# A hybrid attention and RWKV-7 step on one core: three engines in a fixed order through the recurrence, the group norm in four stages, the triangular solve in four pieces

## The chip, the cores and the metric

The kernel runs on one NeuronCore of a Trainium2 chip, on its five engines: TensorE (PE, with its weight loads shown as PEld), VectorE (DVE), ScalarE (ACT), GpSimd (POOL) and SyncE (SP), which here issues nearly all transfers between HBM and the core's memory. The metric is the device time of one execution in microseconds (us), lower is better.

## The reference

One inference step of a two-layer trunk over a prompt of 2048 tokens, with 16 meta tokens in front, and over 8 decode sequences of 4 new tokens. Layer 0 is sliding-window attention, layer 1 is RWKV-7 time mixing. The change touches the last stage of layer 1: the recurrence, the group norm, the gate, the output projection and the last RMS norm.

```python
def wkv_scan(S0, r, w, k, v, a, b):
    # S_t = S_{t-1} diag(w_t) + (S_{t-1} a_t) b_t^T + v_t k_t^T ;  y_t = S_t r_t   (16 heads, S 64 x 64)
...
    S, y = wkv_scan(wkv0, r_h, w_h, k_h, v_h, -kk, kk * a_h)
    mean = jnp.mean(y, axis=-1, keepdims=True)
    var = jnp.mean(jnp.square(y - mean), axis=-1, keepdims=True)
    y = ((y - mean) * lax.rsqrt(var + GN_EPS)).reshape(B, T, R_WIDTH)
    y = y * ln_g + ln_b
    bonus = jnp.sum(r_h * k_h * r_k, axis=-1, keepdims=True) * v_h
    y = (y + bonus.reshape(B, T, R_WIDTH)) * jax.nn.silu(g)
    out = jnp.einsum('btw,wd->btd', y, w_out)
...
    h = h + y                      # residual, then the final rmsnorm(h) * final_gain
```

## The kernel before

The recurrence is done by chunks of 32 tokens. A token tile (`Unit` in the code) is 128 tokens, so four chunks; tile 0 holds the meta tokens in one chunk, tiles 1 to 16 hold the prompt, and the sample tokens run at the end. The attention layer, the projections of layer 1 and the decay factors lie ahead of this stage and leave their results in DRAM.

Inside a chunk, the token-by-token dependence is a triangular system per head. Its inverse is computed ahead, for a whole tile, and does not depend on the state:

- `scores(u, c2)` multiplies keys and queries for two chunks into PSUM (`pz`). ACT copies one part to `LAs` (four copies), DVE multiplies the rest by the masks `smk` back into the tile `L` (four instructions).
- `inverse(u)` writes `LAs` to DRAM (`la_d`), reads it back with the heads on partitions (`LA`), multiplies it by the norms `ln`, and runs 31 steps of two POOL instructions each: `XT` is an outer product, `X` takes it in by a sum. Step j works on (j//2 + 1) x (31 - j) columns. The result goes to DRAM (`tt_d`) and comes back as `TT`.
- `keys(u, c2)` transposes the decayed keys `BK` on PE into `kt`; ACT copies them to `LS` (eight copies).

`chain(u, ch)` is the recurrence proper, in three steps: PE multiplies `L` with `Z` (state and values) into `C`, and ACT copies it to `R0s`; PE multiplies `R0s` with `TT` (the solve) and ACT copies the result into `Z` (four copies); PE multiplies `LS` with `Z`, and DVE scales this into the next chunk's `Z` (four instructions `Z<-C,pe`). The next chunk's first product needs that `Z`. So from chunk to chunk there is one chain through PE, ACT, PE, ACT, PE and DVE.

Between these steps the loop over tiles and chunks gives out other work in small portions, by a budget of estimated microseconds: `project_out` of the tile two back (chunks 0 and 1, dense products `po`), `gate` of the tile one back (chunks 2 and 3, products `pd`, transposes `yps`, the halves `yp`), `group_norm` of the tile one back (chunks 0 and 1), `outputs` (the products `Y`), and `elementwise`, which loads, scores and starts the inverse of the tile two ahead.

`group_norm` sums `Y` on DVE, subtracts the mean, has ACT square (`ysq`), sums the squares, has POOL take the power -1/2 (`var`), and then runs on DVE the product with `var`, `lng`, `lnb`, and for each half a load `vt` of the values, its product with `bont`, and the sum. `project_out` ends with squares on ACT (`sq`), a power on POOL (`ms`) and the final product of `h` on DVE.

Who runs when: the program text gives an order ("traced" below), but a scheduler in the compiler lays out each engine's queue by its own timeline and the text's priorities. Some places bind it: `tc.issue_after(x)` queues what is traced inside it behind instruction x on x's engine, and `released()` does so for the latest chain instruction of each engine. Each engine, and SP's queue of transfers, then works through its queue in order and waits where an operand is not there.

Of the kernel before, what the change touches and what calls it, by code (L numbers as in the profile page):

```python
# [19 lines left out]
P = 128  # L20
D = 1024
KC = 8
# [8 lines left out]
def tile_hybrid_step(ctx: ExitStack, tc: tile.TileContext, a, o, c):  # L31
# [847 lines left out]
    def begin(idx, t, off, n, kind):  # L879
# [6 lines left out]
        u.blk, u.c0 = place[t][0], (place[t][1] + off) // 32  # L886
        return u

    def load_vectors(u):
# [65 lines left out]
    def inverse(u, room=None, ln=None):  # L955
# [62 lines left out]
    with ExitStack() as ph:  # L1018
# [144 lines left out]
        for x, b in enumerate(order):  # L1163
# [39 lines left out]
            if follow is None:  # L1203
# [11 lines left out]
                if nblk > 2:  # L1215
# [3 lines left out]
                    for i, x0, room in ((1, 0, room1), (0, 1024, None)):  # L1219
                        u = us[i]  # L1220
                        u.LAs = las[:64, x0:x0 + 256 * u.nch].rearrange("p (h c g i) -> p h c g i", h=2, g=4, i=32)
                        for c2 in range(u.np):
                            scores(u, c2)
                        inverse(u, room, las[:, x0 + 1024 - 32:x0 + 1024] if i == 0 else las[:, 1536:1568])
# [19 lines left out]
    with ExitStack() as ph:  # L1244
# [7 lines left out]
        SQ = 2  # L1252
        early = [0]

        def banks(u):
# [37 lines left out]

            return 32 * (1 - e + 2 * gh)

        def elementwise(u):
            load = idle() if u.L else load_vectors(u)
            next(load, None)
# [7 lines left out]
            if u.kind != "m":  # L1306
                u.bont = wk.tile([P, 16], F32, name="bont", tag="bont", bufs=4)
                dma(u.bont[:u.n], bo_d[u.idx])
            if u.tt_d is None:
                u.LAs = wk.tile([64, 2, u.nch, 4, 32], F32, name="LAs", tag="LAs", bufs=1)  # L1310
# [4 lines left out]
                inverse(u)  # L1315
            if u.kind != "s":
                u.TT = wp.tile([P, u.nch, 4, 32], F32, name="TT", tag=("sels", "l2t")[u.idx % 2])
            for gh in range(2):
                dma(u.TT[64 * gh:64 * gh + 64].rearrange("p c g i -> p (c g i)"), u.tt_d[:, gh:4:2].rearrange("k q x -> q k x"))
            yield 0.8  # L1320

        Zcount = [0]
# [224 lines left out]

        def group_norm(u):
            n = u.n
            if u.kind == "s":  # L1550
                u.ytm = u.Ys
            else:
                u.ytm = lt.tile([P, 2, 8, 64], F32, name="ytm", tag="ytm", bufs=1)
            y = u.ytm[:n].rearrange("p e g d -> p (e g) d")
# [3 lines left out]
            for e in range(2):  # L1558
                v_.tensor_reduce(out=mean[:n, e * 8:e * 8 + 8], in_=u.Y[e][:n], axis=AX.X, op=ALU.add)
                yield 0.6  # L1560
            v_.tensor_scalar(out=mean[:n], in0=mean[:n], scalar1=1.0 / 64, scalar2=None, op0=ALU.mult)
            if u.kind == "s":
                for e in range(2):
                    tt(v_, u.ytm[:n, e], u.Y[e][:n], mean[:n, e * 8:e * 8 + 8].unsqueeze(2).broadcast_to([n, 8, 64]), ALU.subtract)
            else:
                for x in range(2):
                    for e, ps_ in HS:
                        tt(v_, u.ytm[64 * x:64 * x + 64, e], u.Y[x][ps_],
                           mean[ps_, x * 8:x * 8 + 8].unsqueeze(2).broadcast_to([64, 8, 64]), ALU.subtract)
                    yield 0.9  # L1570
            for e in range(2):
                ysq = wk.tile([P, 8, 64], F32, name="ysq", tag="ysq", bufs=SQ)
                act(ysq[:n], u.ytm[:n, e], AF.Square)
                v_.tensor_reduce(out=var[:n, e * 8:e * 8 + 8], in_=ysq[:n], axis=AX.X, op=ALU.add)
                yield 0.6
            with tc.high_priority(offset=5000):
                g_.tensor_scalar(out=var[:n], in0=var[:n], scalar1=1.0 / 64, scalar2=64e-5, op0=ALU.mult, op1=ALU.add)
                tt(g_, var[:n], var[:n], mhalf[:n], ALU.pow)
            tt(v_, y, y, bc(var), ALU.mult)
            yield 1.1  # L1580
            yf = u.ytm[:n]
            tt(v_, yf, yf, lng[:n], ALU.mult)
            yield 1.1
            tt(v_, yf, yf, lnb[:n], ALU.add)
            yield 1.1
            for e in range(2):
                vt = wk.tile([P, 8, 64], F32, name="vt", tag="ysq", bufs=SQ)
                dma(vt[:n].rearrange("p g d -> p (g d)"), v_d[u.t][u.cols, e, :])
                tt(v_, vt[:n], vt[:n], u.bont[:n, 8 - e * 8:16 - e * 8].unsqueeze(2).broadcast_to([n, 8, 64]), ALU.mult)
                tt(v_, u.ytm[:n, e], u.ytm[:n, e], vt[:n], ALU.add)  # L1590
                yield 1.2

# [5 lines left out]
        def gate_dense(u, ch, room=None):  # L1598

            n = u.n  # L1600
            if ch == 0:
# [8 lines left out]
            u.gt = gt = wk.tile([P, 512], F32, name="gt", tag="ysq", bufs=SQ) if room is None else room[:, ch]  # L1610
# [24 lines left out]
        def project_out(u, ch):  # L1635
# [10 lines left out]
                                   lambda kc, part: u.yp[kc // 4][:, part, kc % 4, :])  # L1646
            stt(h1[:n, sl], ps[:n], 0.5 / WSC, h1[:n, sl], ALU.mult, ALU.add)
            yield MARK
            sq = wk.tile([P, 512], F32, name="sq", tag="ysq", bufs=SQ)
            act(sq[:n], h1[:n, sl], AF.Square, accum_out=u.ssq[:n, ch:ch + 1])  # L1650
            if ch == 1:
                ms = wk.tile([P, 2], F32, name="ms2", bufs=2)
                with tc.high_priority(offset=5000):
                    g_.tensor_scalar(out=ms[:n], in0=u.ssq[:n], scalar1=1.0 / D, scalar2=0.5e-6, op0=ALU.mult, op1=ALU.add)
                    tt(g_, ms[:n, 0:1], ms[:n, 0:1], ms[:n, 1:2], ALU.add)
                    tt(g_, ms[:n, 0:1], ms[:n, 0:1], mhalf[:n, 0:1], ALU.pow)
                stt(h1[:n], h1[:n], ms[:n, 0:1], fg[:n], ALU.mult, ALU.mult)
                if t == 0:
                    dma(o["y_sample"].rearrange("b t d -> (b t) d"), h1[:32])
# [36 lines left out]

        room_v[0] = pf
        PLAN = {(1, 2): [2], (1, 3): [3], (2, 0): [4], (2, 1): [5], (2, 2): [6], (2, 3): [7]}
        side, rests = [], []

        def after_rhs():

            for gen in rests:
                run(gen)
            with released():
                for fn in side:
                    fn()
            del side[:], rests[:]

        def side_work(u, ch, ahead, last):  # L1710
            if u.kind == "p":
# [10 lines left out]
        for i, u in enumerate(us):  # L1722
# [2 lines left out]
            if i > 2:  # L1725
                pe[0], pe[1] = project_out(us[i - 2], 0), project_out(us[i - 2], 1)
            if i > 1:
                norm = group_norm(us[i - 1])
                ew[0] = ew[1] = norm
                pe[2], pe[3] = gate(us[i - 1], 0), gate(us[i - 1], 1)  # L1730
            if i < 2:
                pe = [rest_v] * 4
            soon = i + 3 if i < 1 else i + 2
            ahead = elementwise(us[soon]) if soon < len(us) and i != 1 else idle()
            for ch in range(u.nch):
# [3 lines left out]
                with released() if i == 0 else ExitStack():  # L1739
                    next(rec)  # L1740
                after_rhs()
                run(ew[ch], 1.2)
                run(pe[ch], VB.get((i, ch), (1.2, 1.9))[0])
                next(rec)
# [151 lines left out]
```

## Time and profile before

| | |
|---|---|
| median of 3 runs | 2650.34 us (2645.37 to 2650.36) |
| the profiled execution | 2649.89 us, its span 2648.1 us |
| PE busy | 2243.8 us, 85% of the span |
| DVE busy | 1677.2 us, 63% |
| ACT busy | 1171.9 us, 44% |
| POOL busy | 1042.4 us, 39% |
| first and last copy of a chunk's R0s | at 1609.9 and 2544.0 us |

In rows of a timeline the columns are: start in us, duration in us, engine, line, operation, output and inputs by name, shape, count, and in brackets the idle time before it with what ended it. In rows of waits: engine, line and output, "<-" what it waited for, total us, times, longest. In rows of groups: the busy total and the mean of one in ns, then the idle time before. In rows of windows: the stretch, its length, then busy us and count of PE, PEld, DVE, ACT and POOL, the granted TensorE clock, the DMA share and GB/s. "issue" means that the profile shows nothing that was waited for.

### The profile page before, as it was taken

The page shows a single profiled execution, that of the slowest core. Times are in us where ns is not written, and L with a number is a line of the kernel's source. Part 1 is how long each engine was busy: PE and PEld are TensorE (multiplying, and loading weights), DVE is VectorE, ACT ScalarE, POOL GpSimd, SP SyncE. Part 2 cuts the span into 40 slices and gives each one's busy share as a digit, 9 for nine tenths or more (in the row PEclk, how much of TensorE's full clock was granted, in tenths as well). Part 3 has the DMA queues.
Part 4 walks back from the last instruction along what each step waited for, and adds up shares of the span by engine and source line. Part 5 has one row for each costly group of instructions (what it writes and reads, how often), then busy time and mean ns, then how long its engine had stood idle before and what let it go on. Part 6 is the DMA issues. An engine that isn't in the chain of part 4 may idle for free.

```text
span 2648.1 us, 60911 instructions
## 1 busy us (share of the span) xinstructions
PE 2243.8 (85%) x24932; PEld 1549.0 (58%) x24932; DVE 1677.2 (63%) x3164; ACT 1171.9 (44%) x2799; POOL 1042.4 (39%) x1572
## 2 busy tenths in 40 slices
PE   7999899989999878999999995666777766777797
PEld 5877777768744446777666673444444444444453
DVE  6597666566839877665566665546556556556675
ACT  6676546555514335543434352333334433344332
POOL 4242113331204235433333342345555666556603
PEclk9999999999999989999999997788888988888898
DMA  8433212331466654322222244753444533445323
GB/s 201 126 105 106 81 53 88 120 116 43 156 165 224 208 186 140 98 92 96 85 97 88 77 130 122 203 152 98 112 115 115 143 99 98 117 122 123 85 62 82
DMA packets 346235, 312.99 MB, mean 118 GB/s; under 512 B 205546, under 2 KB 282218, under 8 KB 344131
## 3 DMA queue, kind: packets, MB, share of 16 engines
q1 hardware_dynamic: 344339, 305.30, 39.8%
q0 software_dynamic: 1616, 3.79, 0.6%
q8 instruction: 196, 3.21, 0.5%
q14 instruction: 84, 0.69, 0.1%
HBM read 191.15 MB, written 119.84 MB: 117 GB/s over the span
## 4 chain that ended last, share of the span: by engine, by line
PE 44%; DVE 17%; issue 12%; DMA 9%; ACT 9%; POOL 7%; SPq 3%; POOLq 0%; ACTq 0%; DVEq 0%
PE pd L38 25%; PE po L38 5%; PE C L38 4%; DVE xm L47 3%; DMA L<-ar 3%; SPq L50 3%; PE pz L38 2%; DVE xpr L44 2%; ACT ssb L41 2%; DMA wst<-in_rwkv_w_in 1%; PE sc L38 1%; POOL X L44 1%; PE Y L38 1%; PE oT L38 1%; PE kt L1353 1%
## 5 line engine op out<-in xcount | busy, mean ns | idle before, releaser
L38 PEld LDWEIGHTS <-yp 128*128 128x128 f16 x1488 | 138.5, 98 | 164.1 <-issue 7.5
L47 DVE SCALAR_TENSOR_TENSOR xm<-dx,mu,xn 128x256 f32<-128x256 f32 (+2 forms) x432 | 199.8, 522 | 54.1 <-POOL dx L44 52.9
L38 PE MATMUL C<-Z,L 128*32 128x64 f32 x2048 | 50.1, 249 | 215.5 <-issue 209.2
L44 POOL TENSOR_TENSOR XT<-LA,X 128x126 f32<-128x126 f32 (+24 forms) x458 | 192.7, 421 | 37.9 <-PE C L38 2.5
L44 POOL TENSOR_TENSOR X<-X,XT 128x126 f32<-128x126 f32 (+24 forms) x458 | 186.9, 408 | 34.9
L38 PE MATMUL pd<-wg,xg 128*128 128x512 f16 (+1 forms) x816 | 192.8, 384 | 1.0 <-DMA xg<-xg 1.0
L38 PE MATMUL pd<-xp,wq 128*128 128x256 f16 (+2 forms) x1728 | 184.1, 265 | 9.8 <-DVE qp L47 7.7
L38 PE MATMUL pd<-xp,wg 128*128 128x256 f16 (+2 forms) x1728 | 186.3, 269 | 0.5 <-DVE qp L47 0.4
L38 PE MATMUL pd<-wvv,xpr 128*128 128x512 f16 (+1 forms) x816 | 185.9, 385 | 0.0
L38 PE MATMUL pd<-xpr,w 128*128 128x256 f16 (+2 forms) x1728 | 185.5, 267 | 0.0
L38 PE MATMUL po<-wo,yp 128*128 128x512 f16 x768 | 184.4, 382 | 1.1 <-DVE yp L47 1.0
L38 PEld LDWEIGHTS C<-Z,L 128*32 128x32 f32 x2048 | 39.1, 127 | 240.7 <-issue 239.2
L38 PE MATMUL pd<-xpr,wkk 128*128 128x256 f16 (+2 forms) x1728 | 179.5, 264 | 0.0
L38 PEld LDWEIGHTS <-wq 128*128 128x128 f16 x1728 | 158.4, 98 | 30.4 <-DVE qp L47 8.9
L38 PEld LDWEIGHTS <-wg 128*128 128x128 f16 x1728 | 161.3, 100 | 23.1 <-issue 3.6
L44 POOL TENSOR_TENSOR ssb<-ssb,bias 128x512 f32<-128x512 f32 x64 | 86.3, 1355 | 224.5 <-DVE ssb L462 181.3
L41 ACT ACTIVATE R0s<-C 128x256 f32<-128x256 f32 x65 | 24.9, 383 | 335.0 <-PE C L38 334.3
L38 PEld LDWEIGHTS <-w 128*128 128x128 f16 x1728 | 157.3, 99 | 26.7 <-issue 9.7
L38 PEld LDWEIGHTS <-wkk 128*128 128x128 f16 x1728 | 158.3, 98 | 15.6 <-issue 0.4
L38 PE MATMUL pd<-w,yp 128*128 128x512 f16 x720 | 162.3, 383 | 3.2 <-DMA yp<-y 3.2
L44 POOL TENSOR_TENSOR ps<-wst,ps 128x1024 f16<-128x1024 f32 x32 | 69.4, 2168 | 221.7 <-ACT wst L41 198.3
L44 POOL TENSOR_TENSOR LA<-LA,ln 128x1024 f32<-128x1024 f32 x16 | 31.1, 1947 | 287.1 <-DMA LA<-la_d 240.7
(356 smaller groups left out, 4958.8 us busy)
## 6 DMA issues: line engine op xcount, KB each, us to landing
wst<-in_rwkv_w_in SPq DMA_DIRECT2D x32, 512.0 KB
wsp<-ps SPq DMA_DIRECT2D x32, 512.0 KB
BK<-bk SPq DMA_DIRECT2D x32, 512.0 KB
L<-ar SPq DMA_DIRECT2D x64, 256.0 KB
x<-in_x_prompt SPq DMA_DIRECT2D x29, 512.0 KB
xn<-xn SPq DMA_DIRECT2D x14, 1028.0 KB
ar<-aro SPq DMA_DIRECT2D x28, 512.0 KB
bk<-bko SPq DMA_DIRECT2D x28, 512.0 KB
```

Of the source, the lines that this page charges most:

```text
L38: return t_.matmul(out=out, lhsT=lhsT, rhs=rhs, start=start, stop=stop, **kw).ins
L41: return s_.activation(out=out, in_=in_, func=func, **kw).ins
L44: return e.tensor_tensor(out=out, in0=in0, in1=in1, op=op).ins
L47: v_.scalar_tensor_tensor(out=out, in0=in0, scalar=scalar, in1=in1, op0=op0, op1=op1)
L50: return nc.sync.dma_start(out=out, in_=in_).ins
L1353: t_.transpose(out=ps[:w * 64, j].rearrange("p e d -> p (e d)"), in_=u.BK[half][:, j, 2 * c2:2 * c2 + w, :].rearrange("p c x -> p (c x)"), ...
```

## The change

It rewrites the loop for tiles 2 to 14 (`steady`); tiles 0, 1, 15 and 16 keep the old loop, with small joints.

- `in_order()` is called at the end of every chunk. It ties each traced instruction of DVE, ACT and POOL to the one traced before it on the same engine, so these three run in the order of the text. PE and SP stay with the scheduler.
- `inverse` becomes a generator that stops before steps 8, 16 and 23. For the tile two ahead its first piece is traced in chunk 3, the other three in chunks 0, 1 and 2 of the next tile. The load of `TT` follows the last piece.
- The loads of the tile two ahead are traced in chunk 0 (`BK`, `pe`, `bont`, and the first `L`, unless it was loaded in chunk 3 before) and chunk 1 (the second `L`), its scores in chunks 1 and 2.
- `group_norm` runs in stages. In chunk 3 of the tile itself: the loads of `vt`, the mean of the first half, and the products of `vt` with `bont`. In chunk 0 of the next tile: the second mean, the subtractions, the squares and `var`. In chunk 1: the products with `var` and `lng`. In chunk 2: `lnb` and the sums with `vt`.
- `keys(u, 1)` is traced after the solve of chunk 0, `keys(u.next, 0)` after that of chunk 3.
- The last step of `project_out` is cut: squares and `ms` in chunk 2, the final product of `h` in chunk 3.
- `ysq` and `sq` are written to PSUM instead of SBUF, `vt` and `gt` have buffers of their own, and the scratch for POOL's own transfers shrinks from 4096 to 2048.

```diff
@@ inverse
         for j in range(low, 31):
+            if j in (8, 16, 23):
+                yield
...
@@ group_norm
+            if u.kind != "s":
                 for e in range(2):
+                    vt = wk.tile([P, 8, 64], F32, name="vt", tag="vt", bufs=2)
+                    dma(vt.rearrange("p g d -> p (g d)"), v_d[u.t][u.cols, e, :])
+                    vts.append(vt)
+                yield MARK
...
+                if vts and x == 0:
+                    for e in range(2):
+                        tt(v_, vts[e], vts[e], u.bont[...].broadcast_to([n, 8, 64]), ALU.mult)
+                    yield MARK
...
-                ysq = wk.tile([P, 8, 64], F32, name="ysq", tag="ysq", bufs=SQ)
+                ysq = u.Y[e] if u.kind != "s" else wk.tile([P, 8, 64], F32, name="ysq", tag="vt", bufs=2)
...
+            yield MARK
             tt(v_, y, y, bc(var), ALU.mult)
             yield 1.1
             tt(v_, yf, yf, lng[:n], ALU.mult)
-            yield 1.1
+            yield MARK
             tt(v_, yf, yf, lnb[:n], ALU.add)
...
@@ project_out
-            sq = wk.tile([P, 512], F32, name="sq", tag="ysq", bufs=SQ)
-            act(sq[:n], h1[:n, sl], AF.Square, accum_out=u.ssq[:n, ch:ch + 1])
+            act(ps[:n], h1[:n, sl], AF.Square, accum_out=u.ssq[:n, ch:ch + 1])
...
+                yield MARK
                 stt(h1[:n], h1[:n], ms[:n, 0:1], fg[:n], ALU.mult, ALU.mult)
...
+        def in_order():
+            traced = nc.cur_bb.bb.instructions
+            if seen:
+                start = next(k for k in reversed(range(len(traced))) if traced[k] is seen[0]) + 1
+                for x in traced[start:]:
+                    if x.engine in (mybir.EngineType.DVE, mybir.EngineType.Activation, mybir.EngineType.Pool):
+                        if x.engine in tails:
+                            tc.add_manual_dep(x, tails[x.engine].name, mybir.DependencyInfo(
+                                mybir.DependencyClass.NoSync, mybir.DependencyReason.DATA), reason="in order")
+                        tails[x.engine] = x
+            seen[:] = [traced[-1]]
+
+        def steady(i, u, pe):
+            prev, s = us[i - 1], us[i + 2]
...
+            for ch in range(4):
...
+                rec = chain(u, ch)
+                next(rec)                                   # C, R0s
+                after_rhs()
+                if ch in (1, 2):
+                    with released():
+                        if ch == 1:
+                            new_LAs(s)
+                        else:
+                            outputs(u, 1)
+                        scores(s, ch - 1)
+                run(pe[ch], 1.2)
+                next(rec)                                   # the solve
+                with released():
+                    if ch == 0:
+                        if i > 2:
+                            keys(u, 1)
+                        first = L0s.pop(s.idx, None)
+                        load_BK(s)
+                        s.L.append(first or load_L(s, 0))
+                        small_loads(s)
+                    if ch == 1:
+                        s.L.append(load_L(s, 1))
+                    if ch == 3:
+                        keys(u.next, 0)
+                        if i + 3 < len(us):
+                            L0s[i + 3] = load_L(us[i + 3], 0)
+                        inv[s.idx] = inverse(s)
+                        next(inv[s.idx])
+                    elif us[i + 1].idx in inv:
+                        next(inv[i + 1], None)
+                        if ch == 2:
+                            load_TT(us[i + 1])
+                if ch < 3:
+                    run(norm, to=MARK)
+                else:
+                    norms_[u.idx] = group_norm(u)
+                    run(norms_[u.idx], to=MARK)
+                    run(norms_[u.idx], to=MARK)
+                run(pe[ch], 1.9)
+                next(rec, None)                             # the new Z
+                run(pe[ch], to=MARK)
+                rests.append(pe[ch])
+                if ch == 1 and i > 2:
+                    marked.append(pe[ch])
...
+                in_order()
+            side.append(lambda: outputs(u, 3))
...
-    nc = bacc.Bacc("TRN2", target_bir_lowering=False, num_devices=1, dynamic_dma_scratch_size=4096)
+    nc = bacc.Bacc("TRN2", target_bir_lowering=False, num_devices=1, dynamic_dma_scratch_size=2048)
```

More of the change, by code (lines that the diff above doesn't have):

```diff
@@ L887, in begin, with load_BK, load_L @@
         return u
+    def load_BK(u):
+        u.BK, u.L = [], []
+        for half in range(2):
+            BK = es.tile([P, 4, 4, 64], F32, name="BK", tag="BK", bufs=nbuf["BK"])
+            dma(BK, bk_d[u.blk][:, half * 4:half * 4 + 4, u.c0:u.c0 + u.nch, :])
+            u.BK.append(BK)
+    def load_L(u, c2):
+        L = wl.tile([P, 2, 2, KC, 64], F32, name="L", tag="L", bufs=nbuf["L"])
+        w, c0 = min(2, u.nch - 2 * c2), u.c0 + 2 * c2
+        for e, ps_ in HS:
+            dma(L[ps_, e].rearrange("p c g x -> p (c g x)"), ar_d[u.blk][ps_, c0:c0 + w].rearrange("p c g x -> p (c g x)"))
+        return L
     def load_vectors(u):
@@ L1294, in quad, with small_loads @@
             return 32 * (1 - e + 2 * gh)
-        def elementwise(u):
-            load = idle() if u.L else load_vectors(u)
-            next(load, None)
+        def small_loads(u):
             if u.kind == "s":
@@ L1308, in elementwise, with new_LAs, load_TT @@
                 dma(u.bont[:u.n], bo_d[u.idx])
+        def new_LAs(u):
+            u.LAs = wk.tile([64, 2, u.nch, 4, 32], F32, name="LAs", tag="LAs", bufs=1)
+        def load_TT(u):
+            if u.kind != "s":
+                u.TT = wp.tile([P, u.nch, 4, 32], F32, name="TT", tag=("sels", "l2t")[u.idx % 2])
+            for gh in range(2):
+                dma(u.TT[64 * gh:64 * gh + 64].rearrange("p c g i -> p (c g i)"), u.tt_d[:, gh:4:2].rearrange("k q x -> q k x"))
+        def elementwise(u):
+            load = idle() if u.L else load_vectors(u)
+            next(load, None)
+            small_loads(u)
             if u.tt_d is None:
-                u.LAs = wk.tile([64, 2, u.nch, 4, 32], F32, name="LAs", tag="LAs", bufs=1)
+                new_LAs(u)
                 for c2 in range(u.np):
@@ L1314, in elementwise @@
                     yield 0.8
[L1315 to L1319, printed above, removed]
+                for _ in inverse(u):
+                    pass
+            load_TT(u)
             yield 0.8
@@ L1549, in group_norm @@
             n = u.n
[L1550 to L1554, printed above, removed]
             mean = wk.tile([P, 16], F32, name="mean", tag="mean", bufs=2)
@@ L1557, in group_norm @@
             bc = lambda x: x[:n].unsqueeze(2).broadcast_to([n, 16, 64])
[L1558 to L1562, printed above, removed]
-                for e in range(2):
[L1564 to L1567, printed above, removed]
+            vts = []
@@ new lines, in group_norm @@
+            if u.kind != "s":
+                for e in range(2):
+                    vt = wk.tile([P, 8, 64], F32, name="vt", tag="vt", bufs=2)
+                    dma(vt.rearrange("p g d -> p (g d)"), v_d[u.t][u.cols, e, :])
+                    vts.append(vt)
+                yield MARK
+            for x in range(2):
+                ms_ = mean[:n, x * 8:x * 8 + 8]
+                v_.tensor_reduce(out=ms_, in_=u.Y[x][:n], axis=AX.X, op=ALU.add)
+                v_.tensor_scalar(out=ms_, in0=ms_, scalar1=1.0 / 64, scalar2=None, op0=ALU.mult)
+                if vts and x == 0:
+                    for e in range(2):
+                        tt(v_, vts[e], vts[e], u.bont[:n, 8 - e * 8:16 - e * 8].unsqueeze(2).broadcast_to([n, 8, 64]), ALU.mult)
+                    yield MARK
+                if x == 0:
+                    u.ytm = u.Ys if u.kind == "s" else lt.tile([P, 2, 8, 64], F32, name="ytm", tag="ytm", bufs=1)
+                    y = u.ytm[:n].rearrange("p e g d -> p (e g) d")
+                for e, ps_ in HS:
+                    if u.kind == "s" and e == 0:
+                        tt(v_, u.ytm[:n, x], u.Y[x][:n], ms_.unsqueeze(2).broadcast_to([n, 8, 64]), ALU.subtract)
+                    elif u.kind != "s":
@@ L1609, in gate_dense @@
                                    lambda kc, part: u.xg[:, kc // 2, part, kc % 2, :])
-            u.gt = gt = wk.tile([P, 512], F32, name="gt", tag="ysq", bufs=SQ) if room is None else room[:, ch]
+            u.gt = gt = wk.tile([P, 512], F32, name="gt", tag="gt", bufs=1) if room is None else room[:, ch]
             act(gt[:n], ps[:n], AF.Tanh, scale=0.5 / WSC)
@@ new lines, in steady @@
+        def steady(i, u, pe):
+            prev, s = us[i - 1], us[i + 2]
+            norm = norms_.pop(prev.idx, None)
+            if norm is None:
+                norm = group_norm(prev)
+                run(norm, to=MARK)
+                run(norm, to=MARK)
+            if i == 2:
+                in_order()
+            for ch in range(4):
+                if (i, ch) == (2, 0):
+                    late_consts()
+                rec = chain(u, ch)
[31 more added lines that the diff above has]
+                if ch < 3:
+                    run(norm, to=MARK)
+                else:
+                    norms_[u.idx] = group_norm(u)
[7 more added lines that the diff above has]
+                    marked.append(pe[ch])
+                for part in PLAN.get((i, ch), ()):
+                    with released():
+                        load_w(*((0, w_g, "wg", part) if part < 4 else (1, w_o, "wo", part - 4)))
+                in_order()
+            side.append(lambda: outputs(u, 3))
@@ L1705, in after_rhs @@
+        norms_, L0s, inv = {}, {}, {}
+        def after_rhs():
+            for gen in list(rests):
+                rests.remove(gen)
+                if gen in marked:
+                    run(gen, to=MARK)
+                    marked.remove(gen)
+                    rests.append(gen)
+                else:
+                    run(gen)
             with released():
@@ L1732, in tile_hybrid_step @@
                 pe = [rest_v] * 4
+            if 1 < i < len(us) - 2:
+                steady(i, u, pe)
+                continue
+            if i > 1:
+                ew[0] = ew[1] = norms_.pop(i - 1, None) or group_norm(us[i - 1])
             soon = i + 3 if i < 1 else i + 2
@@ L1741, in tile_hybrid_step @@
                 after_rhs()
+                if i + 1 in inv and i > 1:
+                    with released():
+                        if ch == 0:
+                            keys(u, 1)
+                        next(inv[i + 1], None)
+                        if ch == 2:
+                            load_TT(us[i + 1])
                 run(ew[ch], 1.2)
```

23 lines of the change are left out of this document (11 added, 12 removed).

## The prediction

> **What bounds the kernel now.** I read the page first, then the busy time by stage, then who waited for whom in the recurrence, and last the timeline of one token tile. The profiled execution took 2649.89 us (span 2648.1), against a median of 2650.34; I sum against the profiled one. The three runs (2645.37 to 2650.36) differ by 0.2%, about 5 us: less can't be told from no change.
>
> ```profile
> span 2648.1 us, 60911 instructions
> 1707.52:2440.43 732.91, 528.25 (x9848) 328.68 (x9844) 413.15 (x631) 276.42 (x697) 422.79 (x867) 0.86 0.46 118
> 1707.52 0.38 ACT L41 ACTIVATE R0s<-C 128x256 f32<-128x256 f32 x1 [3.52 <-PE C L38]
> 2440.43 0.38 ACT L41 ACTIVATE R0s<-C 128x256 f32<-128x256 f32 x1
> ```
>
> R0s is copied once per chunk of 32 tokens, so it marks the chunks. The two R0s rows are the first chunk of tiles 2 and 15, and between them lie the 13 tiles that the change rewrites: 732.91 / 13 = 56.4 us per tile. The window row (columns PE, PEld, DVE, ACT, POOL, PEclk) gives per tile PE 40.6, DVE 31.8, ACT 21.3, POOL 32.5. No engine fills 56.4, so waits do. The waits of the window 1720 to 2440 (12.8 tiles) name them:
>
> ```profile
> PE C L38 <- issue: 182.2, 25, 15.6
> DVE ytm L44 <- POOL var L44: 97.8, 13, 17.1
> DVE yp L47 <- ACT yp L41: 68.3, 13, 5.8
> DVE vt L44 <- DMA vt<-v: 67.7, 11, 7.3
> DVE h L47 <- POOL ms L44: 47.9, 12, 4.4
> ```
>
> PE stands still about 14 us per tile ahead of C, the first product of a chunk. The profile names no releaser, but C reads Z, which DVE writes, and DVE runs its queue in order. It stands 281.7 us (22 per tile) on four things that have nothing to do with Z. One tile shows it:
>
> ```profile
> 1922.95 0.38 ACT L41 ACTIVATE R0s<-C 128x256 f32<-128x256 f32 x1 [1.34 <-PE C L38]
> 1932.10 0.38 ACT L41 ACTIVATE R0s<-C 128x256 f32<-128x256 f32 x1
> 1897.47 2.91 POOL L44 TENSOR_TENSOR var<-var,mhalf 128x16 f32<-128x16 f32 x1
> 1900.42 1.45 DVE L44 TENSOR_TENSOR ytm<-ytm,var 128x1024 f32<-128x1024 f32 x1 [9.51 <-POOL var L44]
> 1906.87 1.73 DVE L44 TENSOR_TENSOR Z<-C,pe 64x256 f32<-64x256 f32 x4
> 1908.70 1.08 PE L38 MATMUL C<-Z,L 128*32 128x64 f32 x32 [15.46 <-issue]
> 1909.89 0.38 ACT L41 ACTIVATE R0s<-C 128x256 f32<-128x256 f32 x1 [20.21 <-PE C L38]
> ```
>
> The power of the variance sits in POOL's queue among the triangular solve's steps. DVE waits 9.51 us for it, the masks and norm steps behind it follow, Z is written at 1906.87, and only then C goes. The chunk after it is bounded otherwise: 1909.89 to 1922.95 (13.06), then 9.15 to 1932.10.
>
> **The change, part by part.** Chunks 0 to 3 of a steady tile, by the traced order. Durations:
>
> ```profile
> 1871.24 0.65 PE L38 MATMUL C<-Z,L 128*32 128x64 f32 x32
> 1871.71 1.08 PE L38 MATMUL Y<-Z,L 128*32 128x64 f32 x64
> 1884.92 1.15 PE L38 MATMUL pz<-L,BK 64*64 64x64 f32 x62 [1.96 <-DMA L<-ar]
> 1911.41 1.99 PE L38 MATMUL pz<-L,BK 64*64 64x64 f32 x64
> 1886.01 1.47 PE L38 MATMUL po<-wo,yp 128*128 128x512 f16 x6
> 1887.40 0.65 PE L38 MATMUL C<-R0s,TT 32*32 32x64 f32 x32
> 1887.99 2.12 PE L38 MATMUL po<-wo,yp 128*128 128x512 f16 x9
> 1890.03 1.15 PE L38 MATMUL C<-Z,LS 128*64 128x64 f32 x32
> 1874.19 0.66 PE L1623 MATMUL yps<-ident,gt 128*128 128x128 f32 x4
> 1873.41 3.10 ACT L41 ACTIVATE LS<-kt 64x256 f32<-64x256 f32 x8 [1.01 <-PE kt L1353]
> 1877.17 1.56 ACT L41 ACTIVATE Z<-C 32x256 f32<-32x256 f32 x4
> 1878.63 1.13 ACT L41 ACTIVATE ysq<-ytm 128x512 f32<-128x512 f32 x2
> 1880.88 1.28 DVE L1574 TENSOR_REDUCE var<-ysq 128x8 f32<-128x512 f32 x2
> ```
>
> *Chunk 0.* C 0.65, yps 0.66, Y 1.08, six dense products 1.47, solve 0.65: 4.5. Then ACT copies Z (1.56), and the change puts keys' eight LS copies (3.10) ahead of the squares (1.13) in ACT's fixed order: 10.3. Half of the variance sums (0.64) runs after the last square, then Z on DVE (1.73) and two hand-overs: 13.0. The cover is gone here: PE alone would need about 11. The LS copies no longer stand before yp, so most of yp's 5 us wait goes.
> *Chunk 1.* C, scores 1.15, 1.47, 0.65, 2.12, Z's product 1.15, 2.12: 9.3. DVE has the masks, then the variance product and gain, done before Z's product if var is there.
> *Chunk 2.* From the traced 13.06 I take the cold clock (C 1.08 against 0.65 and scores 1.99 against 1.15 are 1.3 slower right after the stall, and Y between them at their ratio of 1.7 is 0.8 slower: 2.1) and about 1 of PE's wait for Z: 10.0.
> *Chunk 3.* Traced 9.15 plus yps 0.66: 10.0. h's final product waits no longer, as ms is computed a chunk ahead.
> Sum 42.3, against 40.6 of PE work.
>
> Now the waits that remain. *BK and L* move to chunks 0 and 1 (2 and 4 issues per tile, with pe and bont; count unchanged). BK's buffers are freed by chunk 0's transposes, so the scores of chunk 1 may wait as the scores do now (1.96): I take 1.5, between 0 and 6. *vt*: its two loads move ahead of the norm, but the product with bont is traced right behind them, after solve 3. It waits 5.3 per tile now; h, gate and mean stand before it on DVE, so I take 1.0 of 0 to 5.3.
>
> *var* is the main unknown. POOL's order is now fixed: LA times ln and steps 0 to 7 (traced in chunk 3), steps 8 to 15, var (chunk 0), steps 16 to 22 (chunk 1), ms, steps 23 to 30 (chunk 2). What arrives late at its head delays var, and DVE has Z behind it.
>
> ```profile
> 1913.45 1.55 ACT L41 ACTIVATE LAs<-pz 32x256 f32<-32x256 f32 x4 [1.52 <-PE pz L38]
> 1915.02 1.35 SPq L50 DMA_DIRECT2D tt_d<-X  x2
> 1919.74 4.25 SPq L50 DMA_DIRECT2D la_d<-LAs  x2
> 1935.94 1.91 POOL L44 TENSOR_TENSOR LA<-LA,ln 128x1024 f32<-128x1024 f32 x1 [19.75 <-DMA LA<-la_d]
> 1952.35 0.43 POOL L44 TENSOR_TENSOR XT<-LA,X 128x135 f32<-128x135 f32 x1
> ```
>
> The 128x135 row is step 16, the first one behind var in the new order. So LA to var is 1952.35 - 1935.94 = 16.4, and the scale and power add 3.2 (2.91 and the small scale): 19.6. The scores are copied to LAs by 1915.0, 5 us into chunk 2; from the issue of la_d to POOL's start were 16.2. If SP issues la_d as soon as LAs stand, LA starts 21.2 after chunk 2 begins, 11.2 into chunk 3, and var is done at 30.8. DVE reaches it 10.0 + 13.0 + 4.8 (C, scores, four masks) = 27.8 after chunk 3 begins. Wait: 3.0. Nearest ends: 0 (la_d found less traffic) and 7.9 (below). I take 3.0. ms and the last piece then have a chunk to spare.
>
> *Small edits.* ysq and sq go to PSUM, still one ACT instruction each: 0, held PSUM banks up to 0.5 per tile. The mean's scale becomes two, one short DVE instruction more, inside DVE's idle time: 0. SP issues the same transfers. The scratch of POOL's own DMAs is halved: only the sample state's 32 writes in the tail use it (row below; 0.63 us each); 0, at worst 10 once. Tile 2 has its loads among late weights: 0, at worst 10 once. PE is not in the fixed order.
>
> Sum: 42.3 + 1.5 + 1.0 + 3.0 = 47.8 us per tile, 8.6 less than 56.4; times 13 = 112. 2649.9 - 112 = 2538, taken as 2540. Its own range, with var's wait half-way to either end (1.5 to 5.4, so 46.3 to 50.2 per tile), is 2519 to 2570.
>
> **Where a rule speaks against it.**
>
> ```profile
> L44 POOL TENSOR_TENSOR XT<-LA,X 128x121 f32<-128x121 f32 x12 | 13.5, 1123 | 0.9
> L44 POOL TENSOR_TENSOR XT<-LA,X 128x120 f32<-128x120 f32 x24 | 9.6, 400 | 1.9
> L44 DVE TENSOR_TENSOR gt<-gt,ytm 128x512 f32<-128x512 f32 x25 | 25.4, 1015 | 0.9
> L44 DVE TENSOR_TENSOR vt<-vt,bont 128x512 f32<-128x512 f32 x26 | 20.4, 786 | 67.9 <-DMA vt<-v 67.7
> L47 DVE SCALAR_TENSOR_TENSOR h<-h,ms,fg 128x1024 f32<-128x1024 f32 x12 | 15.4, 1284 | 47.9 <-POOL ms L44 47.9
> L1544 POOL DMA_DIRECT2D out_new_wkv_s<-room x32: 620/631/722, 2589.7 to 2634.8; - x32
> ```
>
> Two POOL steps of the same size (121 and 120 columns) last 1123 and 400 ns; the long one falls where DVE wakes for its variance product. The Trainium skill ("SBUF — State Buffer", section "SBUF: two separate sides") says that a VectorE instruction with two SBUF inputs and a GpSimd one share a port pair that is locked for the whole instruction. By that rule the stall that the change removes was GpSimd's free time. What it would do here, from the rows: during the first two pieces DVE now runs h (1.28), gt twice (2.0) and vt twice (1.6): 4.9 us in which POOL stands.
>
> **Rivals.**
> 1. *The GpSimd queue is stretched by DVE.* var comes 4.9 later, a wait of 7.9, 52.7 per tile: 2650 - 13 x 3.7 = 2602. For it: the 1123 ns. Against: only part of the 4.9 falls on POOL's steps. 0.20.
> 2. *It ends slower: SP closes a loop.* Where the scheduler leaves the last piece's tt_d and TT ahead of la_d, as in the rows above (1915.02, 1919.74), SP sits on POOL's result and the next solve starts only after it. A tile is then POOL's 32.5, plus 4.7, plus 16.2: 53.4 (2611). With the stretch of 4.9 it is 58.3, or 2675. It is slower from a stretch of 3.0 on. For it: the traced order puts TT first, and POOL waited 19.75 for LA. Against: la_d is ready first, since the solve starts a chunk later. 0.18, half of it slower.
> 3. *PE's floor is nearly reached*, no remaining var or vt wait: 43.8 per tile, 2486. 0.13.
> 4. *No change*: the stall moves to another DVE wait of the same size, chiefly chunk 0's squares and var: 2650. 0.04.
> My forecast: 0.45.
>
> **How the numbers follow.** Slower: 0.10 (half of rival 2, and a little for the one-time costs). Same: 0.04. Faster: 0.86. The range runs from 2492 to 2625: it takes in my own case, rival 1, the lower half of rival 2 and part of rival 3; left out are the slow half of 2, rival 4 and the lower part of 3, about 0.19.
>
> **What would show it.** Right: R0s of a steady tile at steps near 13, 12, 10, 10 and none over 16; PE's wait before C under 5 us per tile; DVE's waits for ms and yp nearly gone, vt under 2, var 2 to 5; no cold products after the second chunk; POOL's LA about 11 us into chunk 3, and POOL more than 65% busy. Wrong: var's wait of 8 or more (rival 1); la_d on SP behind TT (rival 2); the squares in chunk 0 costing more than 2 beyond PE.

## The result and the profile after

The changed kernel takes 2532.8 us, the median of four runs (2527.51 to 2542.64), against 2648.57 for the kernel before on the same chip: a ratio of 0.9568, with an interval of 0.9537 to 0.96. The profiled execution is the slowest of the four, 2542.64 us.

Page of the changed kernel and its window of tiles 2 to 14, from the first R0s of tile 2 to that of tile 15 (columns as before):

```profile
span 2540.9 us, 60840 instructions
1713.16:2341.65 628.49, 522.65 (x9848) 322.49 (x9844) 408.64 (x649) 274.00 (x698) 432.14 (x877) 0.93 0.54 138
```

The span is 107.2 us shorter. The 13 rewritten tiles took 732.91 and take 628.49: 104.4 of it, 8.0 per tile (56.4 to 48.3). Tile 2 begins 5.6 later (1713.16 against 1707.52), and what follows tile 14 is 8.4 shorter (2540.9 - 2341.65 against 2648.1 - 2440.43). The engines are busy about as long as before (PE 522.65 for 528.25, POOL 432.14 for 422.79); PE's idle time per tile fell from 15.7 to 8.1.

The chunks of one steady tile after, copies of R0s:

```profile
2040.02 0.38 ACT L41 ACTIVATE R0s<-C 128x256 f32<-128x256 f32 x1 [1.51 <-PE C L38]
2049.91 0.39 ACT L41 ACTIVATE R0s<-C 128x256 f32<-128x256 f32 x1 [0.35 <-PE C L38]
2064.74 0.39 ACT L41 ACTIVATE R0s<-C 128x256 f32<-128x256 f32 x1 [3.43 <-PE C L38]
2076.39 0.38 ACT L41 ACTIVATE R0s<-C 128x256 f32<-128x256 f32 x1 [4.61 <-PE C L38]
2087.56 0.38 ACT L41 ACTIVATE R0s<-C 128x256 f32<-128x256 f32 x1 [1.51 <-PE C L38]
```

The first row is chunk 3, the next chunk 0 of the following tile. So the steps are 9.9 for chunk 3, then 14.8, 11.7 and 11.2 for chunks 0, 1 and 2. This tile is near the mean: over tiles 4 to 14 the four chunks took 15.2, 10.8, 11.5 and 10.5 us on average. Chunk 0 varies most, from 11.9 to 16.9, and in three of the 13 tiles (11, 13 and 14) it is over 16. No step of over 20 is left.

Waits of the changed kernel from 1765 to 2341 (12 tiles):

```profile
DVE L L44 <- ACT LAs L41: 79.0, 24, 5.1
DVE yp L47 <- ACT yp L41: 71.8, 24, 6.2
PE C L38 <- issue: 45.6, 32, 3.4
POOL var L1613 <- DVE var L1610: 31.0, 11, 4.3
PE C L38 <- DMA TT<-tt_d: 24.2, 14, 2.5
DVE vt L44 <- DMA vt<-v: 7.5, 8, 1.9
PE pz L38 <- DMA BK<-bk: 3.5, 7, 0.8
DVE ytm L44 <- POOL var L44: 1.8, 1, 1.8
```

PE's unnamed wait ahead of C fell from 14 us per tile to 3.8, DVE's wait for var from 97.8 in all to 1.8. New is PE's wait for TT, 2.0 per tile. GpSimd now waits for DVE's sums, where DVE waited for GpSimd.

The transfers around the solve, from the timeline of the changed kernel:

```profile
2040.19 1.34 SPq L50 DMA_DIRECT2D tt_d<-X  x2
2043.12 1.91 POOL L44 TENSOR_TENSOR LA<-LA,ln 128x1024 f32<-128x1024 f32 x1 [2.95 <-DMA LA<-la_d]
2045.57 1.12 SPq L50 DMA_DIRECT2D TT<-tt_d  x2
2050.90 0.30 PE L38 MATMUL C<-R0s,TT 32*32 32x64 f32 x4 [0.22 <-DMA TT<-tt_d]
2053.71 0.64 PE L38 MATMUL C<-R0s,TT 32*32 32x64 f32 x28 [2.51 <-DMA TT<-tt_d]
2060.05 0.46 POOL L44 TENSOR_TENSOR X<-X,XT 128x128 f32<-128x128 f32 x1
2062.49 2.91 POOL L44 TENSOR_TENSOR var<-var,mhalf 128x16 f32<-128x16 f32 x1
2081.41 1.79 SPq L50 DMA_DIRECT2D la_d<-LAs  x2
2090.75 1.91 POOL L44 TENSOR_TENSOR LA<-LA,ln 128x1024 f32<-128x1024 f32 x1 [3.04 <-DMA LA<-la_d]
```

GpSimd starts a solve (the LA rows) every 47.6 us, and waits only 3 us for its data. The two rows that follow are the same group of instructions on the pages, after and before:

```profile
L44 POOL TENSOR_TENSOR LA<-LA,ln 128x1024 f32<-128x1024 f32 x16 | 31.1, 1946 | 118.5 <-DMA LA<-la_d 92.5 <-DVE X L44 25.9
L44 POOL TENSOR_TENSOR LA<-LA,ln 128x1024 f32<-128x1024 f32 x16 | 31.1, 1947 | 287.1 <-DMA LA<-la_d 240.7 <-DVE Z L44 25.2 <-DMA Z<-v 21.2
```

Ahead of 16 solves GpSimd stood 287.1 us before and 118.5 after. In the kernel before these waits sat in a closed cycle, which the experiments below take apart: a solve ends, SP stores and loads its TT, only then scatters the next tile's scores (la_d), gathers them (LA), and the next solve starts. That the cycle carries most of the difference was tested by closing it in the changed kernel and opening it in one without any tie; it was not tried in the kernel before itself. There the scores were late too, as their chunk followed the wait for var: in the prediction's rows LAs stood at 1915.00, when the solve also ended, so SP's order alone held the scatter back by 4.7 us (to 1919.74). How the gain over that kernel divides between SP's order and the wait for var is therefore open.

### The profile page after: what moved, and what is told of

It reads as the page before. It is cut to its first block, busy times and chain, and to the rows that moved or that the text cites. A ratio compares the mean times of both kernels' runs of the same rounds, so it can differ in the third digit from the quotient of the medians.

```text
span 2540.9 us, 60840 instructions
## 1 busy us (share of the span) xinstructions
PE 2241.2 (88%) x24932; PEld 1545.2 (61%) x24932; DVE 1676.6 (66%) x3181; ACT 1168.9 (46%) x2799; POOL 1050.7 (41%) x1572
## 4 chain that ended last, share of the span: by engine, by line
PE 37%; DVE 21%; DMA 15%; ACT 8%; POOL 8%; issue 7%; SPq 4%; POOLq 0%; ACTq 0%; DVEq 0%
PE pd L38 21%; PE po L38 6%; DVE xm L47 5%; SPq L50 4%; PE C L38 3%; DVE xpr L44 2%; DMA TT<-tt_d 2%; DMA BK<-bk 2%; ACT ssb L41 2%; DMA tt_d<-X 2%; POOL X L44 2%; PE pz L38 2%; DMA wst<-in_rwkv_w_in 2%; PE sc L38 1%; POOL XT L44 1%
## 5 line engine op out<-in xcount | busy, mean ns | idle before, releaser
L44 POOL TENSOR_TENSOR X<-X,XT 128x126 f32<-128x126 f32 (+24 forms) x458 | 200.9, 439 | 35.6
L44 POOL TENSOR_TENSOR XT<-LA,X 128x126 f32<-128x126 f32 (+24 forms) x458 | 183.6, 401 | 36.2 <-issue 2.5
L38 PE MATMUL po<-wo,yp 128*128 128x512 f16 x768 | 193.3, 395 | 0.0
L44 DVE TENSOR_TENSOR L<-pz,smk 64x512 f32<-64x512 f32 x128 | 88.1, 689 | 96.7 <-ACT LAs L41 94.7
L38 PEld LDWEIGHTS <-xpr 128*128 128x128 f16 (+1 forms) x816 | 78.8, 100 | 102.1 <-issue 16.4
L44 DVE TENSOR_TENSOR xpr<-xm,xpr 128x512 f16<-128x512 f32 (+2 forms) x144 | 99.0, 709 | 56.7 <-ACT xpr L41 56.3
L41 ACT ACTIVATE ssb<-ssb,ng 128x128 f32<-128x128 f32 (+1 forms) x272 | 104.2, 384 | 57.3 <-DVE es L44 53.6
```

What stands on the lines that cost most here:

```text
L38: return t_.matmul(out=out, lhsT=lhsT, rhs=rhs, start=start, stop=stop, **kw).ins
L41: return s_.activation(out=out, in_=in_, func=func, **kw).ins
L44: return e.tensor_tensor(out=out, in0=in0, in1=in1, op=op).ins
```

## The experiments

Each edit is against the changed kernel unless it says otherwise, and each ratio is to the kernel before.

**No ties.** All three engines go back to the scheduler; layout, pieces and stages stay.

```diff
-                    if x.engine in (mybir.EngineType.DVE, mybir.EngineType.Activation, mybir.EngineType.Pool):
+                    if x.engine in ():
```

> The new layout by chunks without the ties: the scheduler places var 2 to 3 solve steps further back in GpSimd's queue (as many steps behind LA as in the kernel before), and DVE meets the product with var ahead of its masks. Theory A, the layout gives the gain because the solve starts a chunk earlier: var is done about 2.5 us later and DVE reaches it about 5 us earlier, so a wait of 3 to 4 us per tile, part of it hidden: 1 to 2 us per tile, 2545 to 2570 us. Theory B, the fixed order gives the gain: the 15 us stall before C returns, 2620 us or more.

2674.18 us, ratio 1.0105 (1.0075 to 1.0134): 1% slower than before, in theory B's range. The layout by itself gives nothing. Among the waits from 1790 to 2340 the largest on DVE was a new one:

```profile
DVE vt L44 <- DMA vt<-v: 129.3, 16, 15.3
```

**The ties alone.** The kernel before with the same ties in tiles 2 to 14 (a call of `in_order()` per chunk), in its own traced order.

```diff
+            if i == 2:
+                in_order()
...
+                if 1 < i < len(us) - 2:
+                    in_order()
```

> The kernel before with DVE, ACT and GpSimd tied to the traced order in tiles 2 to 14, nothing else changed. var then stands behind all 31 solve steps instead of 18. Theory A: var comes about 11 us later, with DVE's queue and Z behind it, so about 67 us per tile and 2780 us (2740 to 2820). Theory B: the order alone is worth most of the gain, under 2600 us.

2779.31 us, ratio 1.0497 (1.0467 to 1.0528), as expected. In that order var stands behind all 31 steps, and DVE pays (waits from 1790 to 2340):

```profile
DVE ytm L44 <- POOL var L44: 155.1, 8, 20.1
```

**The solve whole.** One cut ahead of the last step, so that nearly all of the solve is traced in chunk 3, ahead of var.

```diff
-            if j in (8, 16, 23):
+            if j == 30:
```

> The new kernel with the solve traced in one go in chunk 3 (only its last step in the next chunk), so that var stands behind 30 steps and not 16. Theory A: LA starts 3 us into chunk 3, the steps end 33 us later and var 36.5 us later, while DVE reaches the product with var about 27 us after chunk 3 begins: a wait of about 13 us, less the 2.5 us wait for TT, which now comes early. 58 us per tile, 2660 to 2690 us. Theory B, the pieces are of no account: within 15 us of the new kernel's 2533.

2646.31 us, ratio 0.9991 (0.9975 to 1.0007): the whole gain is gone, though a little less bad than expected. So with ties, the pieces are needed: they put var behind 16 steps instead of 30. SP has tt_d and TT ahead of la_d here as well, but that doesn't hold the scatter back: TT goes at 2070.77, LAs stand at 2080.81 and la_d follows at 2082.89. The same wait as in the last kernel is back:

```profile
DVE ytm L44 <- POOL var L44: 106.9, 10, 16.1
```

**Later cuts.** The solve is cut behind steps 9, 18 and 26, to finish sooner and bring TT in time.

```diff
-            if j in (8, 16, 23):
+            if j in (9, 18, 26):
```

> The new kernel with the solve cut at steps 9, 18 and 26 instead of 8, 16 and 23: GpSimd works in the time in which it now waits for DVE before var and for ACT before ms, and the last piece is 5 steps and not 8, so TT arrives 3 to 4 us earlier. Theory A, the wait for TT is what is left over (24 us in 12 tiles on TensorE, and everything behind it in chunk 0): 2 to 2.5 us per tile, 2500 to 2508 us. Rival, another wait of chunk 0 (squares, sums, Z) takes its place at once: 2526 to 2536 us.

2534.95 us, ratio 0.9579 (0.9546 to 0.9612): no change, as the rival had it. PE's wait for TT went, but PE's unnamed wait ahead of C rose from 38.8 to 77.2 (both from 1790 to 2340). The scheduler placed tt_d between la_d and the load of LA, and TT between the two loads of vt; DVE waited longer for vt (38.0 where it was 7.5):

```profile
DVE vt L44 <- DMA vt<-v: 38.0, 12, 4.6
```

**Ties on GpSimd alone.**

```diff
-                    if x.engine in (mybir.EngineType.DVE, mybir.EngineType.Activation, mybir.EngineType.Pool):
+                    if x.engine in (mybir.EngineType.Pool,):
```

> The new kernel with GpSimd alone tied to the traced order, DVE and ACT left to the scheduler. In this build SP's queue again has la_d ahead of tt_d and TT, and the vt loads ahead of LA, as in the new kernel; without any tie it had tt_d and TT first and vt last. Theory C, what the ties are worth is GpSimd's order and the SP order that follows from it: 2540 to 2570 us. Theory B, DVE's order is what counts: 2620 us or more, as without ties.

2520.33 us, ratio 0.9516 (0.9495 to 0.9536): the best kernel of the study, below theory C's range and 12 us under the changed one; the two intervals just miss each other. Ties on DVE and ACT are not needed. Timeline:

```profile
2035.77 1.91 POOL L44 TENSOR_TENSOR LA<-LA,ln 128x1024 f32<-128x1024 f32 x1 [4.18 <-DMA LA<-la_d]
2071.22 1.57 SPq L50 DMA_DIRECT2D la_d<-LAs  x2
2077.72 1.35 SPq L50 DMA_DIRECT2D tt_d<-X  x2
2082.06 1.91 POOL L44 TENSOR_TENSOR LA<-LA,ln 128x1024 f32<-128x1024 f32 x1 [4.37 <-DMA LA<-la_d]
```

SP has la_d ahead of tt_d, and the next solve starts 4.3 us after the last one's store, 46.3 after its start. SP is not tied here; its order differs from that of the kernel without ties, though only GpSimd's order was fixed.

**No ties, the late vt product.** Without ties, and the product of vt with bont moved back to just ahead of the sums: is the vt wait what made the untied kernel slow?

```diff
-                    for e in range(2):
-                        tt(v_, vts[e], vts[e], u.bont[:n, 8 - e * 8:16 - e * 8].unsqueeze(2).broadcast_to([n, 8, 64]), ALU.mult)
...
+                    tt(v_, vt, vt, u.bont[:n, 8 - e * 8:16 - e * 8].unsqueeze(2).broadcast_to([n, 8, 64]), ALU.mult)
...
+                    if x.engine in ():
```

> No ties, and the products of vt with bont moved back to just ahead of the sums with vt (chunk 2 of the next tile), the loads where they are, so that DVE no longer meets vt before it has landed. Theory C: the wait for vt (129 us in about 10 tiles) was the stall that came back without ties; it goes, and what is left is SP's loop (tt_d, TT, la_d, LA, solve), about 53 us per tile: 2580 us (2550 to 2620). Theory B: another wait takes its place at once and it stays over 2640 us.

2662.75 us, ratio 1.0056 (1.0034 to 1.0079): a miss of theory C by over 80 us, in theory B's range. The vt wait is gone, and DVE waits about as long for var. GpSimd shows why nothing was won:

```profile
DVE ytm L44 <- POOL var L44: 142.1, 9, 17.0
2167.97 1.91 POOL L44 TENSOR_TENSOR LA<-LA,ln 128x1024 f32<-128x1024 f32 x1 [19.87 <-DMA LA<-la_d]
2226.43 1.91 POOL L44 TENSOR_TENSOR LA<-LA,ln 128x1024 f32<-128x1024 f32 x1 [19.73 <-DMA LA<-la_d]
```

The period is 58.5 us: the solve ends at 2205.5, 37.5 after its start, and tt_d (issued at 2205.54), TT (2208.87), la_d (2210.56) and LA (2219.73) take the other 20.9. Where DVE stands in the meantime, at vt or at var, is only where the cycle's slack shows up. That gave the theory of the loop, which the last runs test.

**Z ahead of the norm stage.** The chunk's last product and `Z<-C,pe` are traced ahead of the norm stage instead of behind it, against the 1.5 us that PE waits for Z.

```diff
+                run(pe[ch], 1.9)
+                next(rec, None)
                 if ch < 3:
...
-                run(pe[ch], 1.9)
-                next(rec, None)
```

> The new kernel with each chunk's part of the group norm traced behind the chain's last step instead of ahead of it, so that Z on DVE is no longer behind norm work. In the new kernel Z ends 1.5 and 1.4 us after TensorE has run out of work in chunks 0 and 2 and 0.3 to 0.4 us in the others, and DVE idles 6 us per tile later for LAs. Theory D, DVE's order in the chunk bounds the tile: 3.7 us per tile, 2485 us (2475 to 2500). Rival, TT and so GpSimd's loop bounds it: 2522 to 2540 us.

2548.51 us, ratio 0.9622 (0.9599 to 0.9645): if anything slower than the changed kernel, a miss. The variance sums come later on DVE, and GpSimd, which has half a solve queued behind var, waits for them (31.0 in the changed kernel from 1790 to 2340):

```profile
POOL var L1613 <- DVE var L1610: 88.9, 11, 10.7
```

**Both of these**, Z first and the later cuts.

```diff
-            if j in (8, 16, 23):
+            if j in (9, 18, 26):
...
+                run(pe[ch], 1.9)
+                next(rec, None)
                 if ch < 3:
```

> The same with the solve cut at steps 9, 18 and 26. Theory D with the wait for TT as the second bound: 2 us per tile less than with the old cuts, 2455 to 2475 us. Rival, the cuts move only the wait (as they did alone): equal to the run before within 8 us.

2558.71 us, ratio 0.9663 (0.9634 to 0.9692), again a miss. In both I had priced PE's waits and not GpSimd's. For var, ms and LA together GpSimd waits 100.4 us in the changed kernel, 110.8 with Z first and 133.0 with both edits (all from 1790 to 2340); in the last it is chiefly LA (78.4, with 54.1 for var), as SP has tt_d between its two loads. That these waits set the time was read from the traces and not tested.

**The loop opened on SP alone.** No ties. The scatter, the gather and the loads of ln and X are traced in chunk 2, right behind the scores, and the last tt_d of the solve before is queued on SP behind them.

```diff
+                        if ch == 2:
+                            inv[s.idx] = inverse(s)
+                            next(inv[s.idx])
...
-                        next(inv[i + 1], None)
+                        with tc.issue_after(s.la_in) if ch == 2 else ExitStack():
+                            next(inv[i + 1], None)
```

> No engine keeps the traced order (DVE, ACT and GpSimd are left to the scheduler, as in the kernel without ties that gave 2674 us); the only further edit is on the transfer queue: the inverse's scatter, its gather back and the factor's broadcast are traced in chunk 2 right behind the scores, and the last tt_d store of the solve before is put behind the next LA load on SP, so that the solve no longer ends ahead of the next tile's scatter. Theory (the loop solve, TT store and load, scatter, gather, solve sets the period): the solves overlap the transfers again and the time is 2565 us (2540 to 2590), some 110 us under the kernel without ties. Rival (the order of GpSimd, or of DVE and ACT, is what counts by itself): at least 2640 us.

2555.19 us, ratio 0.9635 (0.9606 to 0.9664), as the loop gave: 119 us less than the same layout without ties. No engine is tied in it. Timeline:

```profile
2052.39 1.91 POOL L44 TENSOR_TENSOR LA<-LA,ln 128x1024 f32<-128x1024 f32 x1 [9.92 <-DMA tt_d<-X]
2090.18 1.27 POOL L44 TENSOR_TENSOR X<-X,ln 128x512 f32<-128x512 f32 x1
2092.29 0.98 SPq L50 DMA_DIRECT2D la_d<-LAs  x2
2099.09 1.34 SPq L50 DMA_DIRECT2D tt_d<-X  x2
2102.45 1.91 POOL L44 TENSOR_TENSOR LA<-LA,ln 128x1024 f32<-128x1024 f32 x1 [9.80 <-DMA LA<-la_d]
```

The scatter no longer waits for the solve's result, and tt_d stands behind it. The solve ends at 2091.45 and the scatter goes at 2092.29; in the tile before it went at 2041.11, 0.2 ahead of the solve's end. GpSimd waits 9.8 instead of 20 and the period is 50.1.

**The loop closed on SP.** All ties stay; in chunk 3 the next scatter is queued on SP behind the load of TT.

```diff
+                u.tt_in = dma(u.TT[64 * gh:64 * gh + 64].rearrange("p c g i -> p (c g i)"), u.tt_d[:, gh:4:2].rearrange("k q x -> q k x"))
...
-                        next(inv[s.idx])
+                        with tc.issue_after(us[i + 1].tt_in) if i + 1 in inv else ExitStack():
+                            next(inv[s.idx])
```

> The changed kernel with all its ties, and one edit: in chunk 3 the scatter of the next inverse is put behind the TT load of the present one on SP's queue, so that a solve has to end before the next one's transfers start. Theory (the loop): the period is the solve's length in the kernel without ties and with the late vt product, 37.5 us, and the transfers' 20.9, together 58.4 us per tile against 48.3, so 2664 us (2645 to 2680). Rival (what counts is where GpSimd's queue has the group norm's variance, which this edit leaves): under 2570 us.

2650.3 us, ratio 0.9995 (0.998 to 1.001): the whole gain gone by the order of transfers alone, 14 less than expected. Timeline:

```profile
2040.83 1.91 POOL L44 TENSOR_TENSOR LA<-LA,ln 128x1024 f32<-128x1024 f32 x1 [17.76 <-DMA LA<-la_d]
2079.30 2.51 SPq L50 DMA_DIRECT2D tt_d<-X  x2
2083.76 1.12 SPq L50 DMA_DIRECT2D TT<-tt_d  x2
2084.97 3.16 SPq L50 DMA_DIRECT2D la_d<-LAs  x2
2098.68 1.91 POOL L44 TENSOR_TENSOR LA<-LA,ln 128x1024 f32<-128x1024 f32 x1 [19.41 <-DMA LA<-la_d]
```

38.5 of solve and 19.4 of transfers make a period of 57.9. LAs stood at 2070.68, so the order on SP held the scatter back by 14.3. The rival (var's place in GpSimd's queue is what counts) falls: its place among the steps is that of the changed kernel. Here la_d took 13.7 to become LA, against 9.3 in the changed kernel.

**Ties on DVE and ACT alone.**

```diff
+                    if x.engine in (mybir.EngineType.DVE, mybir.EngineType.Activation):
```

> DVE and ACT keep the traced order and GpSimd is left to the scheduler. SP then has the TT store and load ahead of the next tile's scatter, and the variance stands 21 steps behind the start of the solve on GpSimd. Loop theory: 2640 to 2690 us, as without any tie. Rival (DVE's and ACT's order carries the gain): 2570 us or less.

2652.51 us, ratio 0.9996 (0.9985 to 1.0007), as the loop gave. SP has tt_d (2080.13) and TT (2083.51) ahead of la_d (2086.42), and GpSimd's period is 57.6:

```profile
2043.83 1.91 POOL L44 TENSOR_TENSOR LA<-LA,ln 128x1024 f32<-128x1024 f32 x1 [19.59 <-DMA LA<-la_d]
2086.42 3.30 SPq L50 DMA_DIRECT2D la_d<-LAs  x2
2101.46 1.91 POOL L44 TENSOR_TENSOR LA<-LA,ln 128x1024 f32<-128x1024 f32 x1 [20.16 <-DMA LA<-la_d]
```

**Ties on GpSimd alone, with later cuts.** The best kernel, cut behind steps 9, 18 and 26.

```diff
-            if j in (8, 16, 23):
+            if j in (9, 18, 26):
...
+                    if x.engine in (mybir.EngineType.Pool,):
```

> The kernel in which GpSimd alone keeps the traced order (2520 us), with the solve cut behind steps 9, 18 and 26 instead of 8, 16 and 23, so that the solve ends up to three steps sooner in chunk 0. Theory (TT's lateness is what remains in chunk 0): 1.5 us per tile less, 2500 us (2492 to 2512). Rival (another wait takes its place, as in the changed kernel with these cuts): no change, 2515 to 2528 us.

2568.99 us, ratio 0.9677 (0.9657 to 0.9698): slower by 49 us than with the old cuts, a miss that neither side expected. SP's order changed once more (tt_d between la_d and the load of LA); two waits grew, on PE from 27.4 and on DVE from 16.1 (1790 to 2340):

```profile
PE yps L1663 <- DVE gt L44: 70.4, 13, 8.0
DVE vt L44 <- DMA vt<-v: 52.5, 11, 6.3
```

Which of SP's changes does it was not tried. The place of tt_d alone doesn't explain it: with the same cuts and all ties SP had tt_d at that place too, and lost nothing.

## Why the prediction was right, and where it was not

It said 47.8 us per steady tile, and 48.3 were measured; 2540, and the median is 2532.8. The total agrees better than its terms, whose errors offset each other; that part was luck. Of the signs named for being right, some failed: chunk 0 went over 16 in three tiles, the wait for yp stayed, and the clock fell in chunk 3 of three tiles (7, 11 and 12, each granted 0.85).

- *The stall that goes.* Right in place: DVE's wait for var is nearly gone, and PE's wait ahead of C fell from 14 to 3.8 us per tile. The reading was incomplete in depth. I took POOL's 19.75 us ahead of LA for spare time of an idle engine and held a closed loop for a rival to come. It was there already: from one start of a solve to the next (1877.32 to 1935.94) 19.75 of 58.6 us were this wait, and the solve with var and ms had the rest, 38.9. The runs that close the loop land where the kernel before is (2650.3 and 2652.51), whichever wait DVE then shows.
- *Rival 2* therefore had the right mechanism with a price too low: 53.4 per tile without a stretch, where the closed loop measured 57.6 to 58.5. The mis-sized term is POOL's 32.5: that is busy time, and from a solve's start to its end, with var, ms and the gaps between dependent steps, it takes 36.3 (tied DVE and ACT) to 38.5. In the changed kernel the reason given against it held: la_d goes out 5.0 us into chunk 2 (2081.41 against R0s at 2076.39), ahead of tt_d, as predicted.
- *var, 3.0 per tile*: measured 1.8 us in all. The term that failed is the 16.2 us from la_d to POOL's start, taken from a scatter caught in the loop; it took 9.3. So LA starts 3.1 us into chunk 3 and not 11.2, and var is done 25.4 into it (2065.40) and not 30.8, nearly always before DVE asks.
- *"ms and the last piece then have a chunk to spare"* was false for the last piece. The solve ends at 2040.2 and tt_d is issued at 2040.19, but TT only at 2045.57, behind vt and the landing of tt_d, and PE can go on at 2053.71, after a wait of 2.51. I had put no price on it: 2.0 per tile. In chunk 0 it pushes the transposes, yp, the squares and the sums back with it.
- *Chunk 0*, 13.0, took 14.8: TT's wait, and Z on DVE at 2062.14 behind all of the variance sums and not behind half.
- *Chunk 1*, 9.3 and a share of the waits, took 11.7 in the tile shown: its scores went in two halves with 0.8 of waiting for BK, and six dense products took 2.49 instead of 1.47 at a lower granted clock (below). The clock explains little of it, since chunk 1 of the tile before took 11.1 at full clock. *Chunk 2* took 11.2 for 10.0, *chunk 3* 9.9 for 10.0.
- *BK and L*, 1.5, cost 0.3 per tile on PE; *vt*, 1.0, cost 0.6. The wait for yp was to go for the most part; it was 5.3 per tile and is 6.0 (71.8 / 12). In chunk 0 of the tile shown it is 4.58 (at 2055.60): PE's wait for TT holds back the transposes that yp needs, and the squares, the sums and Z follow behind it on DVE. What it costs by itself was not separated.
- *Rival 1*, GpSimd stretched by DVE by 4.9: from LA's start to the end of step 15, 17.4 (2043.12 to 2060.51) for the 16.4 of before: 1.0. DVE's products meet few of GpSimd's steps. *Rival 3*, PE's floor, was not reached: 8.1 of PE's time per tile are still idle.
- *Outside the sum*: the last tiles became 8.4 shorter, and tile 2 began 5.6 later in the profiled execution.

What carries the gain, then, is that the next solve's scatter no longer stands behind the last solve's result on SP. With ties it has a condition: var must not stand behind the whole solve (the runs with the ties alone and with the solve whole). That is no gain over the kernel before, where var already stood in the middle, behind steps 0 to 18. The ties on GpSimd's order bring SP's order about; those on DVE and ACT bring nothing that could be seen. Why the scheduler turns SP's queue round with GpSimd's order wasn't looked into.

## What to carry to other kernels

An idle engine is spare only if its wait isn't part of a cycle: follow its result through the queues, and where they lead back to its own next start, the period is busy time plus waits, and removing the wait that another engine shows only moves it. Where a scheduler orders a transfer queue, read that queue's order again after every edit: cuts moved by one to three steps changed it here, in a kernel that became 49 us slower (the cause was not isolated). Take a transfer's time from a place whose neighbours on the queue are those it will have.

## What the runs showed of the hardware

Two rows are of use. First, the granted clock of PE was low after short pauses in some tiles. In chunk 0 PE waited 2.5 us for TT and 1.5 for Z, and then (window of chunk 1, and a row in it):

```profile
2064.74:2076.39 11.65, 10.60 (x208) 5.96 (x208) 7.65 (x11) 4.00 (x12) 8.24 (x15) 0.85 0.20 36
2067.08 2.49 PE L38 MATMUL po<-wo,yp 128*128 128x512 f16 x6
```

Granted were 0.85 in this chunk, and six products took 2.49 us that take 1.47 elsewhere, while chunks 0 and 2 had a full clock (1.00). In the tile before, with 1.2 us of waiting for TT and the same 1.5 for Z, it stayed at 1.00 in all four chunks. That the pauses cause it was not tested; if so, part of a wait's price falls on the chunk after it. Second, a GpSimd step beside a DVE instruction:

```profile
2034.46 0.28 POOL L44 TENSOR_TENSOR XT<-LA,X 128x56 f32<-128x56 f32 x1
2034.77 1.22 DVE L44 TENSOR_TENSOR ytm<-ytm,lnb 128x1024 f32<-128x1024 f32 x1
2034.82 1.34 POOL L44 TENSOR_TENSOR X<-X,XT 128x56 f32<-128x56 f32 x1
```

Of two steps on 56 columns the one that meets the DVE product lasts 1.34 us and ends 0.17 us after the product. The Trainium skill ("SBUF — State Buffer", section "SBUF: two separate sides") says that the one of the two that starts first has the shared port pair for its whole instruction; the rows agree. The 17.4 us from LA to the end of step 15 hold three such long steps (0.78, 0.62 and 0.85 us, beside DVE's products of vt and gt) and are 1.0 longer than the 16.4 of before.
